# Where the mixer's output product keeps its incoming weights and its reloaded activations

## The chip, the cores and the metric

The kernel runs on one core of a Trainium2 chip. A core has a matrix engine (PE, with its weight loads listed apart as PEld), a vector engine (DVE), a scalar engine (ACT), GpSimd (POOL) and SyncE (SP), which here only issues DMAs. Each engine takes its own instructions in the order in which the program has them; between engines there are semaphores. On-chip memory is SBUF (128 partitions) and PSUM, into which PE writes. The metric is the device time of one execution in microseconds (us).

## The reference

One inference step of a two-layer decoder, on 512 prompt rows and 64 sample rows (576 columns here, in two halves of 288), with the same float32 weights. Layer 0 runs two mixers side by side, an RWKV-7 time mixer (8 heads) and a retention (8 heads), and adds their joint output product to the residual:

```python
y = jnp.concatenate([ya, yb], axis=-1).astype(x.dtype) @ w_out
x = layer_norm(ALPHA * x + y, ln1_g[l], ln1_b[l])
x = layer_norm(ALPHA * x + sqrelu_mlp(x, w_up[l], w_down[l]), ln2_g[l], ln2_b[l])
```

Layer 1 has a gated short convolution as its mixer and the same MLP. Outputs are both sequences and the new states. The product `@ w_out` (1024 x 1024) is what this document is about.

## The kernel before

**Products.** Every float32 operand is split into a high part and a rest (`hi` by a cast on ACT, `lo` by a subtraction on DVE or POOL), and one product is three matmuls, hi x hi, hi x lo and lo x hi (`mm3`, L152 to L154).

**The stage.** The mixers run as twelve generators that `drive` steps in a written order, `SCHEDULE`, with a priority for each step: the projections (0), preparation, staging, inverse, scan and output of four pairs of RWKV heads (1 to 6), their sample rows (7), four pairs of retention heads in a front and a back half (8 to 10), and the output product `wout` (11). A planner at build time then lists each engine's instructions by these priorities and by the times at which its cost model has their inputs ready. So the order on an engine depends on what an instruction has to wait for in the plan.

**The sets.** Two sets of tiles hold what a pair of RWKV heads works on: `ls` (9 x 3 x 64 values per partition, of which `la` and `sv` are views), `lr` (2 x 9 x 2 x 64), `uv` and small ones (`new_set`). Pairs 0 and 2 use the first set, pairs 1 and 3 the second. After pair 2 nothing in the mixers uses the first set any more. The scan's products at L907 are the last that read its `la`.

**The output product** (class `Wout`). The 1024 inputs come as eight tiles y0 to y7 of 128 x 576: y0 to y3 from the RWKV pairs, y4 to y7 from the retention pairs (`ret0` to `ret3`). y0 and y1 are stored in DRAM as Y0 and Y1 and loaded again. `WP` says which inputs go together and what they wait for:

- part 0: y0, y1, y2, after the projections and pair 2 (`ya2`);
- then `means`, which loads the weights of inputs 6 and 7 (eight loads, summed on DVE, L1363), and then those of input 7 again (four loads), takes the mean off and splits them (L1371 to L1373) for the y7 product of the next stage;
- part 1: y3, y4, y5, after `ya3`, `ret0`, `ret1`; then `center`, which takes the mean off the residual tiles x (products L1385, sixteen subtractions on DVE, L1386);
- part 2: y6, after `ret2`.

In a part, each input is cast (L1397, ACT) and its rest taken (L1398, POOL). Then for each of eight blocks m of 128 outputs the weights are loaded by SP (`weights`, L1340 or L1343), cast (L1346, ACT) and subtracted (L1347, POOL), multiplied into two PSUM tiles `wa`, one for each half of the columns, and added to x on DVE (L1413, L1415). Part 2 runs four `weights` for two blocks each.

Where these tiles live: a weight load goes to `wr`, of which pool `wq` has two, its parts to `wh` and `wl` (shown as h and l in the profile), two each. A place is free again when the cast and the subtraction that read it are done. Y0 and Y1 are loaded into `stg` (L1395), one tile, through which all spills of the projections go to DRAM as well (L1061 to L1063). Pool `wq` lies in memory that held the projections' inputs, and is open once these are read for the last time.

**The next stage.** When the mixers' pools close, new ones open on their memory: `raw3` for incoming weights, `wspa` for split ones, `tmp`, and `hp`, which holds constants, the split y7 (`T.hs[7]`, L1599 and L1600) and later activations. In a partition, the sets have bytes 131,264 to 175,808 and `hp` has 91,424 to 156,992. The y7 product and the first layer norm's sums (L283 to L294) follow; the y7 product uses PSUM that `center` leaves.

**Queues.** SP issues, in its order, the weights of the projections and of the output product, spills, reloads, the small copies of the inverse (L811, L814), and the trunk's weights (L59). POOL issues the residual x (L1504, eight loads) when the projections are through.

The functions that the diff touches and their callers, with line numbers of the profile:

Of the kernel before, what the change touches and what calls it, by code (L numbers as in the profile page):

```python
# [10 lines left out]
F32 = mybir.dt.float32  # L11
F32R = mybir.dt.float32r
# [4 lines left out]
P = 128  # L17
NT = 576
# [6 lines left out]
class Trunk:  # L25
    def __init__(self, tc, w_all, wbufs=9, rawbufs=3, ahead=5):
        self.tc, self.nc, self.w_all = tc, tc.nc, w_all
        self.ahead = ahead
        self.nu = w_all.shape[0]
        self.raw, self.split = {}, {}  # L30
        self.loaded = self.done = 0
        self.halves = False
        self.tb, self.wb = 8, 8
        self.cap = 2 * self.nu - 1
        self.pairs = set()
        self.allocs = 0
        self.chunk = 8
        self.spots = {}
        self.gate = []
        self.gated = 0  # L40
        self.direct = False
        self.kfirst = True
        self.half = None
# [1282 lines left out]
class Wout:  # L1326


    def __init__(self, T, w):
        self.T, self.nc, self.w = T, T.nc, w  # L1330
        self.w7, self.less = [], {}
        self.y = [None] * 8

    def weights(self, m, k0, n):

        t = self.wq.tile([P, 2, P], F32, tag='wr', name='wr', bufs=2)
        b = self.less.get(k0)
        if b is None:
            t = t[:, 0:n]
            self.nc.sync.dma_start(t.rearrange('p m c -> p (m c)'), self.w[30 + m, :, P * k0:P * (k0 + n)])  # L1340
        else:
            n = 2
            self.nc.sync.dma_start(t, self.w[30 + m:32 + m, :, P * k0:P * (k0 + 1)].rearrange('m p c -> p m c'))  # L1343
            self.nc.scalar.activation(t, t, AF.Identity, bias=b)
        hi, lo = (self.wq.tile([P, 2, P], F32R, tag=f'w{c}', name=c, bufs=2)[:, 0:n] for c in 'hl')
        self.nc.scalar.copy(hi, t)  # L1346
        self.nc.gpsimd.tensor_tensor(out=lo, in0=t, in1=hi.bitcast(F32), op=ALU.subtract)  # L1347
        return hi, lo

    def means(self):  # L1350


        nc = self.nc

        def load(k, m):
            t = self.wq.tile([P, 2, P], F32, tag='wr', name='wr', bufs=2)
            nc.sync.dma_start(t, self.w[30 + m:32 + m, :, P * k:P * (k + 1)].rearrange('m p c -> p m c'))
            return t
        for k in (6, 7):
            s = self.wq.tile([P, 4], F32, name=f's{k}', bufs=1)  # L1360
            for m in range(0, 8, 2):
                t = load(k, m)
                nc.vector.tensor_reduce(out=s[:, m // 2:m // 2 + 1], in_=t, axis=AX.XY, op=ALU.add)  # L1363
            b = self.wq.tile([P, 1], F32, name=f'b{k}', bufs=1)
            nc.vector.tensor_reduce(out=b, in_=s, axis=AX.X, op=ALU.add)
            nc.vector.tensor_scalar(out=b, in0=b, scalar1=-1.0 / 1024, scalar2=None, op0=ALU.mult)
            self.less[k] = b
        for m in range(0, 8, 2):
            t = load(7, m)
            hi, lo = (self.wq.tile([P, 2, P], F32R, name=f'k{c}{m}', bufs=1) for c in 'hl')  # L1370
            nc.scalar.activation(t, t, AF.Identity, bias=b)  # L1371
            nc.scalar.copy(hi, t)
            nc.gpsimd.tensor_tensor(out=lo, in0=t, in1=hi.bitcast(F32), op=ALU.subtract)  # L1373
            self.w7 += [(hi[:, x], lo[:, x]) for x in range(2)]
# [48 lines left out]
def build(tc, i, o, coff):  # L1423
    nc = tc.nc
    T = Trunk(tc, i['w'], ahead=2)
    with ExitStack() as es:
# [9 lines left out]
        with ExitStack() as s1:  # L1436
            M = Mixers(T, i, o, coff)
# [31 lines left out]
            for k in range(KT):  # L1469
                t = (M, M1)[k // 4].lr.rearrange('p a b c d -> p (a b c d)')[:, NT * (k % 4):NT * (k % 4 + 1)]  # L1470
# [94 lines left out]
                    if n == 1: W.center(mxb)  # L1565
            rt = {}
            W = Wout(T, i['w'])
            W.sp, W.stage = M.sp, lambda: M.e('stg')
            RF = copy.copy(R)
            R.mx = (M.mx, mxb)[RMX]  # L1570
            drive(tc, projs(), pres(), stages(), back(0), back(1), back(2), back(3), samples(), ret_fronts(), ret_backs((0, 2)), ret_backs((1, 3)), wout())
# [219 lines left out]
```

## Time and profile before

| what | before |
|---|---|
| median of 3 timed runs | 1565.62 us (1565.36 to 1569.27) |
| profiled execution | 1561.02 us |
| its span, first to last instruction | 1559.2 us |
| mean granted TensorE clock | 0.970 |
| PE busy | 1471.8 us (94%) |
| DVE, ACT, POOL busy | 1073.9, 644.8, 546.1 us |
| last projection's end, first layer norm's first sums | about 353 and 517 us |

The page gives busy time by engine and in forty slices, the chain of work that ended last, and the costliest groups of instructions; other views list stretches of time, waits, and single instructions with what released them. "A <- B" with three numbers is a wait of A for B: us in total, times, the longest. A timeline row is start, length, engine, line, operation, tiles, count, and in brackets the idle time before it with its releaser. In a row of a stretch the engines come as PE, PEld, DVE, ACT, POOL, each with its busy us and its count.

### The profile page before, as it was taken

To read this page: it belongs to the slowest core of one execution; us is meant where nothing else is said; L and a number is where in the kernel's file an instruction comes from. 1 tells how busy PE (TensorE), PEld (TensorE's weight loads), DVE (VectorE), ACT (ScalarE), POOL (GpSimd) and SP (SyncE) were. 2 spreads that over 40 slices of the span, in tenths; PEclk is the share of its full clock that TensorE was granted. 3 is DMA by queue.
4 is the path that set the end of the run, shared out by engine and by line. 5 is a ranking of instruction groups with operands and counts; after the bars stand their busy time and mean duration, and the time that the engine had idled before them with its cause. 6 is when DMAs were issued, how large, how long until landed. Compare 5 with 4: busy or idle time off the path is not lost.

```text
span 1559.2 us, 29833 instructions
## 1 busy us (share of the span) xinstructions
PE 1471.8 (94%) x11744; PEld 1421.0 (91%) x11744; DVE 1073.9 (69%) x2040; ACT 644.8 (41%) x1355; POOL 546.1 (35%) x619
## 2 busy tenths in 40 slices
PE   6999999998888999999999988999998999999995
PEld 6999898987777889999999988899998999999995
DVE  4656766765756994755747779899799475574755
ACT  4434323332233761432525445444366243251533
POOL 2032213345432350211203466555573030221355
PEclk9999999999979999999999999999999999999998
DMA  5333234435223032241422402222303223132211
GB/s 170 98 97 91 86 96 134 140 92 164 84 73 130 12 104 77 68 131 55 123 68 82 137 14 68 82 78 101 122 1 110 81 72 119 55 122 69 90 60 61
DMA packets 73244, 141.08 MB, mean 90 GB/s; under 512 B 21744, under 2 KB 33248, under 8 KB 73104
## 3 DMA queue, kind: packets, MB, share of 16 engines
q1 hardware_dynamic: 70272, 130.74, 26.8%
q0 software_dynamic: 1536, 5.57, 1.1%
q10 hardware_dynamic: 1296, 2.86, 0.5%
q8 instruction: 92, 1.51, 0.4%
q14 instruction: 48, 0.39, 0.1%
HBM read 125.44 MB, written 13.70 MB: 89 GB/s over the span
## 4 chain that ended last, share of the span: by engine, by line
PE 73%; DVE 11%; DMA 5%; issue 4%; POOL 4%; ACT 2%; SPq 1%; DVEq 0%; ACTq 0%; POOLq 0%
PE acc L152 20%; PE acc L153 20%; PE acc L154 20%; DVE wl L78 3%; PE mx L835 2%; DMA raw<-in_w 2%; DMA wr<-in_w 1%; DVE u L341 1%; PE mx L732 1%; PE wa L152 1%; PE wa L154 1%; DVE hl L78 1%; PE wa L153 1%; PE mx L574 1%; POOL ts L1643 1%
## 5 line engine op out<-in xcount | busy, mean ns | idle before, releaser
L77 ACT CAST wh<-raw 128x512 fp32r<-128x512 f32 x440 | 252.7, 618 | 420.7 <-PE acc L153 267.8
L78 DVE TENSOR_TENSOR wl<-raw,wh 128x512 fp32r<-128x512 f32 x440 | 333.6, 790 | 41.9 <-ACT wh L77 35.1
L153 PE MATMUL acc<-hl,wh 128*128 128x288 f32 x1180 | 348.9, 297 | 0.0
L154 PE MATMUL acc<-hh,wl 128*128 128x288 f32 x1180 | 348.6, 296 | 0.0
L152 PE MATMUL acc<-hh,wh 128*128 128x288 f32 x1180 | 346.3, 297 | 2.0 <-DVE ta L205 1.8
L152 PEld LDWEIGHTS acc<-hh,wh 128*128 128x128 f32 x1180 | 221.2, 188 | 2.9 <-DVE ta L205 2.0
L153 PEld LDWEIGHTS acc<-hl,wh 128*128 128x128 f32 x1180 | 222.2, 188 | 0.5
L154 PEld LDWEIGHTS acc<-hh,wl 128*128 128x128 f32 x1180 | 222.2, 188 | 0.3
L152 PE MATMUL acc<-xh,wh 128*128 128x288 f32 x480 | 147.5, 309 | 14.5 <-ACT xh L1472 12.8
L123 POOL TENSOR_TENSOR s<-raw 128x512 f32<-128x512 f32 x37 | 53.1, 1435 | 268.6 <-DMA raw<-in_w 205.4
L153 PE MATMUL acc<-xl,wh 128*128 128x288 f32 x480 | 145.6, 304 | 0.0
L154 PE MATMUL acc<-xh,wl 128*128 128x288 f32 x480 | 145.5, 303 | 0.0
L153 PE MATMUL acc<-lt,wh 128*128 128x288 f32 x444 | 131.2, 296 | 4.7 <-DVE lt L78 4.7
L154 PE MATMUL acc<-ht,wl 128*128 128x288 f32 x444 | 131.5, 296 | 0.9 <-DVE wl L78 0.9
L152 PE MATMUL acc<-ht,wh 128*128 128x288 f32 x444 | 131.0, 295 | 0.0
L123 POOL TENSOR_TENSOR raw<-raw 128x512 f32<-128x512 f32 x37 | 54.9, 1485 | 160.6 <-DVE raw L123 106.7
L152 PEld LDWEIGHTS acc<-xh,wh 128*128 128x128 f32 x480 | 90.7, 190 | 17.9 <-ACT xh L1472 13.2
L152 PE MATMUL acc<-ho,wh 128*128 128x288 f32 x352 | 104.7, 298 | 0.5 <-DVE tb L205 0.5
L154 PE MATMUL acc<-ho,wl 128*128 128x288 f32 x352 | 105.0, 299 | 0.0
L153 PE MATMUL acc<-lo,wh 128*128 128x288 f32 x352 | 105.0, 298 | 0.0
L153 PEld LDWEIGHTS acc<-xl,wh 128*128 128x128 f32 x480 | 90.9, 189 | 2.5 <-DVE xl L1473 0.7
L154 PEld LDWEIGHTS acc<-xh,wl 128*128 128x128 f32 x480 | 91.0, 190 | 1.5 <-issue 0.2
(485 smaller groups left out, 3478.4 us busy)
## 6 DMA issues: line engine op xcount, KB each, us to landing
raw<-in_w SPq DMA_DIRECT2D x160, 512.0 KB, 3.6
raw<-in_w SPq DMA_DIRECT2D x60, 256.0 KB, 2.9
wr<-in_w SPq DMA_DIRECT2D x32, 128.0 KB, 2.2
A<-stg SPq DMA_DIRECT2D x9, 288.0 KB, 2.4
x<-in_x POOLq DMA_DIRECT2D x8, 288.0 KB, 7.8
out_y<-x SPq DMA_DIRECT2D x16, 144.0 KB, 1.8
kr<-A SPq DMA_DIRECT2D x6, 288.0 KB, 2.7
lr<-in_x ACTq DMA_DIRECT2D x4, 288.0 KB
```

What stands on the lines that cost most here:

```text
L77: a = self.nc.scalar.copy(hi[:, s], src[:, s])
L78: b = self.nc.vector.tensor_tensor(out=lo[:, s], in0=src[:, s], in1=hi[:, s].bitcast(F32), op=ALU.subtract)
L123: tt = lambda e, o, x, y, op: e.tensor_tensor(out=o, in0=x, in1=y, op=op)
L152: nc.tensor.matmul(acc, lhsT=hi, rhs=xh, start=first, stop=False)
L153: nc.tensor.matmul(acc, lhsT=hi, rhs=xl, start=False, stop=False)
L154: nc.tensor.matmul(acc, lhsT=lo, rhs=xh, start=False, stop=last)
L341: nc.vector.tensor_tensor(out=u, in0=r, in1=mn, op=ALU.subtract)
L574: self.nc.tensor.matmul(ps, lhsT=lhsT, rhs=rhs[:, o:o + n], start=True, stop=True)
L732: nc.tensor.matmul(both[h][:, i], lhsT=b3[q, c, h:h + 2].rearrange('p s t -> p (s t)'), rhs=la[q, c], start=True, stop=True)
L835: nc.tensor.matmul(ps[:, i], lhsT=bd(self.mb if n < 3 else self.Y0, j + i), rhs=v[:, j + i], start=True, stop=True)
L1643: (nc.vector if n in SUMV else nc.gpsimd).tensor_tensor(out=t(n), in0=a, in1=b, op=ALU.subtract)
```

## The change

The output product gets places in the first set's tiles. `slot()` cuts the set's `ls` into six pieces of 256 values (pieces of chunks 0 to 7; chunk 8 lies behind them) and hands them out in turn, to `weights` and to the loads of `means` alike: each load takes the next piece, whoever had it. `stage()` cuts the first 1152 values of `lr` into two tiles of 576, one each for Y0 and Y1. The two `wr` tiles go, and the split halves h and l get three tiles each in place of two, so `wq` keeps its size. `stg` is left to the spills. What is computed, and every instruction, stays.

```diff
@@ class Wout
         self.w7, self.less = [], {}
+        self.slots = self.staged = 0
         self.y = [None] * 8
 
+    def slot(self):
+
+        i, self.slots = self.slots % 6, self.slots + 1
+        return self.set.ls.rearrange('p a b c -> p (a b c)')[:, 256 * i:256 * (i + 1)].rearrange('p (m c) -> p m c', c=P)
+
+    def stage(self):
+        i, self.staged = self.staged, self.staged + 1
+        return self.set.lr.rearrange('p a b c d -> p (a b c d)')[:, NT * i:NT * (i + 1)]
+
     def weights(self, m, k0, n):
 
-        t = self.wq.tile([P, 2, P], F32, tag='wr', name='wr', bufs=2)
+        t = self.slot()
...
-        hi, lo = (self.wq.tile([P, 2, P], F32R, tag=f'w{c}', name=c, bufs=2)[:, 0:n] for c in 'hl')
+        hi, lo = (self.wq.tile([P, 2, P], F32R, tag=f'w{c}', name=c, bufs=3)[:, 0:n] for c in 'hl')
...
         def load(k, m):
-            t = self.wq.tile([P, 2, P], F32, tag='wr', name='wr', bufs=2)
+            t = self.slot()
             nc.sync.dma_start(t, self.w[30 + m:32 + m, :, P * k:P * (k + 1)].rearrange('m p c -> p m c'))
@@ build
             W = Wout(T, i['w'])
-            W.sp, W.stage = M.sp, lambda: M.e('stg')
+            W.sp, W.set = M.sp, M
```

## The prediction

> **What bounds the kernel now.** I read the page first, then the busy times by stretch (columns: stretch; length; busy time and count of PE, PEld, DVE, ACT, POOL; granted TensorE clock; DMA share; GB/s), then who waited for whom, the chain of waits, and the timeline of single engines.
>
> ```profile
> span 1559.2 us, 29833 instructions
> PE 73%; DVE 11%; DMA 5%; issue 4%; POOL 4%; ACT 2%; SPq 1%; DVEq 0%; ACTq 0%; POOLq 0%
> 361.00:366.00 5.00, 0.26 (x2) 0.16 (x1) 0.76 (x2) 0.88 (x2) 0.80 (x3) 0.71 0.95 357
> 366.00:376.00 10.00, 10.00 (x92) 9.69 (x92) 4.33 (x7) 2.13 (x8) 3.96 (x4) 0.80 0.27 79
> 416.00:429.00 13.00, 13.00 (x172) 11.44 (x170) 10.64 (x32) 3.10 (x11) 4.74 (x10) 1.00 0.22 69
> 441.00:454.00 13.00, 8.07 (x46) 6.24 (x46) 8.32 (x26) 7.44 (x22) 8.15 (x11) 0.52 0.30 96
> 454.00:463.00 9.00, 9.00 (x41) 8.37 (x41) 2.65 (x9) 0.89 (x3) 1.66 (x4) 0.55 0.11 37
> 463.00:478.00 15.00, 15.00 (x149) 13.48 (x149) 5.95 (x15) 3.51 (x9) 3.87 (x7) 1.00 0.19 61
> 478.00:494.00 16.00, 14.82 (x92) 12.82 (x90) 9.86 (x28) 6.77 (x16) 5.67 (x10) 1.00 0.36 113
> 494.00:501.00 7.00, 2.12 (x9) 1.48 (x9) 7.00 (x19) 5.24 (x12) 1.43 (x2) 0.90 0.61 201
> ```
>
> PE is on 73% of the chain that ends last, and it is full nearly everywhere. The stage that the change touches is an exception: between the last projection (353 us) and the first layer norm (517 us) there are stretches in which PE starves. In 361 to 366 it starts 2 matmuls in 5 us, in 441 to 454 it starts 46 in 13 us, where the 13 us before 429 held 172; in 494 to 501 it starts 9. Behind the second starved stretch the clock is 0.55 for another 9 us, with PE busy throughout. So this stage is bounded by what PE waits for, and by the slow clock that follows such waits. Two chains of waits carry the first two gaps; the third belongs to vector work (below).
>
> ```profile
> PE wa L152 <- ACT hi L1397: 5.6, 2, 4.7
> ACT hi L1397 <- DMA stg<-Y: 9.3, 2, 6.9
> 353.48 3.99 DMA g<-stg
> 357.53 7.56 DMA stg<-Y
> 429.36 2.20 DMA wr<-in_w
> ...
> 450.94 2.29 DMA wr<-in_w
> 453.25 0.41 ACT h L1346
> 453.71 0.61 PE wa L152
> ```
>
> The first gap: the reload of Y0 uses tile `stg`, which must first give up its last spill (g, landed at 357.5). The reload then takes 7.56 us, and the head of PE's queue is a product that waits for its cast. The second gap: the two `wr` buffers take the twelve loads of `means` and then part 1's first weights almost one at a time, from 429.36 to 453.25, and part 1 starts at 453.71.
>
> **The change part by part.** *Activations (two places).* Removed: the wait for `stg`. Moved: two 288 KB loads, earlier on SP. They need Y0 and Y1, stored long before, and the set's `lr`.
>
> ```profile
> 329.86 0.28 PE L907 MATMUL po<-la 64*64 64x64 f32 x4
> 342.06 3.76 SPq L814 DMA_DIRECT2D Y<-d  x8
> 353.04 0.35 SPq L1340 DMA_DIRECT2D wr<-in_w  x1
> 353.31 4.27 POOL L1504 DMA_DIRECT2D x<-in_x  x8 [4.51 <-PE acc L154]
> ```
>
> The row at 329.86 is pair 2's last product over its set; from 330.1 on the six weight places are free too. So both reloads and six weight loads can be issued before 353.04, when the first of them is issued today (the memory of `wr` belongs to the projections' inputs until then). The big x loads (from 353.31), which today run against the Y0 load, come after them. The casts still need `wq`'s memory, so they start at 353. I count all of PE's wait on those casts, 5.6 us (two waits, 4.7 and 0.9): **-5.6**, bounds 0 (another operand is late at the same place) and -5.6. The clock in the 10 us behind is 0.80; at full clock this is 2.0 us less. I take half, **-1.0**, bounds 0 and -2.0, since ret work in it waits for ACT and DMA too.
>
> *Weights (six places, three pairs of split halves).* No instruction is added or taken away. Removed: the wait of a load for the second last user. Each load still has its landing, cast and subtraction; nothing of these gets shorter, they only overlap. Part 1 then starts when its last input is split, not when its weights arrive:
>
> ```profile
> 442.27 0.67 ACT L1397 CAST hi<-tw 128x576 fp32r<-128x576 f32 x1 [0.32 <-DVE tw L1198]
> 443.84 1.40 POOL L1398 TENSOR_TENSOR lo<-tw,hi 128x576 fp32r<-128x576 f32 x1
> ```
>
> That subtraction (y of retention pair 1) ends at 443.84 + 1.40 = 445.24; against 453.71 this is **-8.5**. Bounds: -10.8 (to the end of the last cast, 442.27 + 0.67 = 442.94), and 0, if the retention work of 441 to 454 and not part 1 is what the end waits for. I take -8.5 because from 463 to 494 PE is busy 15.00 of 15 and 14.82 of 16 us: behind the gap the stage is made of PE's own work, and what starts earlier ends earlier.
>
> *Clock.* 9.00 us at 0.55 would be 4.95 at 1.00: -4.05 if the pause before it is filled. Part of it stays (retention operands are late there too), so **-2.0**, bounds 0 and -4.05.
>
> ```profile
> 456.00:459.00 3.00, 3.00 (x16) 3.00 (x16) 0.00 (x0) 0.00 (x0) 0.00 (x0) 0.50 0.08 25
> 459.00:462.00 3.00, 3.00 (x14) 3.00 (x14) 1.12 (x4) 0.41 (x1) 0.18 (x1) 0.50 0.14 46
> ```
>
> [...] The trace has the half clock still in 459 to 462 with PE busy 3.00 of 3 us since 456, so I keep the rows.
>
> *Memory of the set.* Added: the first set is now read until part 2's last weight subtraction, and pool `hp` of the next stage (split y7, constants) lies over part of the sets. A new pool waits for whole old pools, as here, where the first trunk load goes 0.03 us after the last operation on mixer memory (488.12 + 0.76 = 488.88):
>
> ```profile
> 488.12 0.76 DVE L1198 SCALAR_TENSOR_TENSOR y<-y,hd 128x576 f32<-128x576 f32 x1
> 488.91 0.33 SPq L59 DMA_DIRECT2D raw<-in_w  x1
> 488.92 0.67 ACT L1599 CAST hh<-y 128x576 fp32r<-128x576 f32 x1
> 489.68 0.84 DVE L1600 TENSOR_TENSOR hl<-y,hh 128x576 fp32r<-128x576 f32 x1 [0.43 <-ACT hh L1599]
> 494.40 5.91 DVE L1386 TENSOR_TENSOR x<-x,mx 128x288 f32<-128x288 f32 x16
> 500.41 0.58 PE acc L152
> 509.08 0.74 POOL L1347 TENSOR_TENSOR l<-wr,h 128x256 fp32r<-128x256 f32 x1
> 516.59 0.81 DVE L289 TENSOR_TENSOR x<-x,acc 128x288 f32<-128x288 f32 x2
> ```
>
> Today the split of y7 runs at 488.92 to 490.52, and its products start at 500.41, when the 16 centring subtractions leave DVE and PSUM free (494.40 + 5.91 = 500.31). After the change the split waits for the last subtraction of weights. With three pairs of halves only the fourth load must wait, for the products of m = 0 and 1, two adds and 12 products (0.4 and 0.13 us each, rows here and in rival two), some 2.4 us behind 500.31. Cover: DVE has the sixteen adds of part 2 (as the last adds in the fence, 0.81 for two, so 6.5 us) before it misses the y7 products. If the last subtraction stayed at 509.08 + 0.74, the products would begin at 509.82 + 0.67 + 0.84 = 511.33, and 16 adds on DVE of about 0.4 us end at 517.7 or later, 0.3 to 3 us behind today's 517.40. I take **+2.0**, bounds 0 and +3.
>
> *SP and order.* Eight DMAs of 0.35 us move ahead of 353 on SP, past the projections' last weights and spills and the small copies of the inverse: 8 x 0.35 = 2.8 us of SP time. SP is through with those copies at 342.06 + 3.76 = 345.82, and 7.2 us are left to 353.04, so I take 0, bounds 0 and +2.8. On PE, part 0's products become ready earlier and stand among those of pair 3: **+2.0**, bounds 0 and +19 (rival two).
>
> Sum: -5.6 - 1.0 - 8.5 - 2.0 + 2.0 + 0 + 2.0 = **-13.1 us**. The profiled execution took 1561.02 us (span 1559.2 and 1.82 around it), so 1547.9 on its scale. The median of the three timed runs, 1565.62, is 4.6 above it; my prediction goes by the median: 1565.62 - 13.1 = **1552.5 us**.
>
> **Rivals.** *One: only the activations count.* Part 1's early start is swallowed, because its products and the retention pairs share PE, and retention pair 3 (end 488.88) then sets the end. For: the y7 split and the first trunk load both wait for it. Against: the y7 products start 11.5 us after it. Time: -5.6 plus 1.0 of order, 1561.0.
>
> *Two: the products overtake the chain, slower.* Place: PE, 361 to 441. Part 0 is 8 x 3 x 2 x 3 = 144 products; at a step of 0.13 us that is 19 us.
>
> ```profile
> 474.71 0.29 PE L154 MATMUL wa<-hi,l 128*128 128x288 f32 x1
> 474.84 0.29 PE L153 MATMUL wa<-lo,h 128*128 128x288 f32 x1
> ```
>
> Today they trickle in as weights come. If all of them stand ahead of pair 3's inverse and scan and of retention pair 1, they fill the first gap, so that the chain gains nothing there, and the inputs of part 1 come up to 19 us later: 445.24 + 19 = 464.2 against 453.71, +10.5, less the 2.0 of the clock: +8.5, 1574. It decides from 8.5 us of products, some 65, ahead of the chain. For: they were throttled by two buffers only. Against: the written order spreads them between the chain's steps.
>
> *Three: the six places act as one.* If a write to one place waited for readers of the others, every load of part 1 would take its landing (2.20 in the chain above), cast and subtraction one after the other (medians, with 0.390 and 0.724 us, in the rows below): 3.3 us, and 16 of them 53 us against the 40.7 from 453.71 to 494.40 today: +12, 1578. Against: at the start four loads into parts of the same kind of tile (`lr`) are issued in 2.31 us without waiting for each other:
>
> ```profile
> L1346 ACT CAST h<-wr x36: 283/390/407, 355.2 to 509.0; 128x256 fp32r<-128x256 f32 x20, 128x128 fp32r<-128x128 f32 x16
> L1347 POOL TENSOR_TENSOR l<-wr,h x36: 447/724/1203, 360.5 to 510.5; 128x256 fp32r<-128x256 f32 x20, 128x128 fp32r<-128x128 f32 x16
> ...
> 3.52 2.31 POOL L1471 DMA_DIRECT2D lr<-in_x  x4
> ```
>
> **How the numbers follow.** Forecast 0.54, own range 1544 to 1560; better still (all gains at their bounds, -5.6 - 2.0 - 10.8 - 4.05 = -22.45, 1543) 0.04; rival one 0.22; two 0.16; three 0.04. The range leaves out rivals two and three and takes in one with some noise: 1542 to 1568. Under 0.3% (4.7 us) a measurement of this kernel cannot be told from no change. Faster by more: 0.54 + 0.04 and 0.09 of rival one, 0.67. Within: 0.11 of rival one and 0.02 of two, 0.13. Slower: the rest, 0.20.
>
> **What would show it.** Right: reloads of Y0 and Y1 and the first weights issued before 353; no wait of products on their cast at 361 to 366; the twelve loads of `means` in flight several at a time; part 1's first product within 2 us of its last split input; clock 1.0 behind it; the y7 split late, its cost under 3 us. Wrong: part 1's inputs later than 445 (rival two), first products of y7 waiting for their split while DVE idles (memory term), the trunk's start unmoved although part 1 starts earlier (rival one), one load in flight at a time (rival three), or projections that wait for SP before 353.

## The result, and the profile after

| | before | after |
|---|---|---|
| median of the timed runs | 1565.61 us (1565.36 to 1569.27, 4 runs) | 1545.97 us (1545.34 to 1548.84, 4 runs) |
| profiled execution | 1561.02 us | 1545.83 us |
| its span | 1559.2 us | 1544.1 us |
| mean granted TensorE clock | 0.970 | 0.972 |

The ratio is 0.9882, with a 95% interval of 0.9858 to 0.9905: about 18.5 us, or 1.2%, faster. The forecast was 1552.5, so the change gave more than its sum of 13.1 us. The two profiled executions differ by 15.2 us. The rest of the difference of the medians comes from the execution that was profiled before, which lies 4.6 us under its own median; no trace shows those microseconds, so the accounts below are made on the profiles' 15.2. Lines of Wout are ten higher in the kernel after (L1425 is L1415 of before, L1396 is L1386, L1609 is L1599; L1611 where y7 has a memory of its own), and from here on "pair 3" means the last retention pair (`ret3`), which makes y7; its last step is L1198.

The kernel after: the page's span and chain by engine, then the busy times of stretches as before (stretch; length; busy time and count of PE, PEld, DVE, ACT, POOL; granted clock; DMA share; GB/s):

```profile
span 1544.1 us, 29826 instructions
PE 73%; DVE 11%; issue 5%; POOL 4%; DMA 4%; ACT 2%; SPq 1%; DVEq 0%; ACTq 0%; POOLq 0%
```

```profile
361.00:366.00 5.00, 5.00 (x40) 4.71 (x39) 2.77 (x7) 0.77 (x2) 5.00 (x6) 0.83 0.92 331
366.00:376.00 10.00, 10.00 (x110) 9.55 (x109) 6.54 (x12) 3.42 (x12) 5.14 (x8) 1.00 0.49 136
441.00:454.00 13.00, 13.00 (x110) 11.38 (x109) 6.44 (x17) 2.52 (x8) 5.85 (x8) 1.00 0.14 43
454.00:463.00 9.00, 9.00 (x102) 7.87 (x102) 3.37 (x7) 3.63 (x10) 1.22 (x3) 1.00 0.18 52
463.00:478.00 15.00, 9.85 (x78) 8.70 (x73) 11.47 (x27) 3.46 (x10) 5.08 (x7) 0.91 0.08 27
478.00:494.00 16.00, 13.95 (x70) 12.48 (x71) 13.08 (x35) 4.51 (x10) 2.15 (x6) 0.66 0.29 102
```

PE's and DVE's shares of the chain, 73% and 11%, are what they were, so the shares alone tell nothing of this change. The two starved stretches of before are full: 361 to 366 holds 40 matmuls in place of 2, 441 to 454 holds 110 in place of 46, and 454 to 463 runs at a clock of 1.00 in place of 0.55. The clock of 0.83 in 361 to 366 is taken up again below. But a hole has opened further back. From 463 to 478 PE is busy 9.85 of 15 us, where it was full, and from 478 to 494 its clock is 0.66, where it was 1.00.

The kernel after, who waited for whom on PE from 350 to 505 us (total, times, longest), then SP's timeline where the reloads and the first weights are issued, with pair 2's last product over its set on PE:

```profile
PE wa L152 <- DVE x L1425: 6.8, 1, 6.8
```

```profile
316.75 0.38 SPq L1405 DMA_DIRECT2D lr<-Y  x1
317.18 5.30 SPq L1350 DMA_DIRECT2D la<-in_w  x4
322.59 0.51 SPq L1405 DMA_DIRECT2D lr<-Y  x1
332.15 0.28 PE L907 MATMUL po<-la 64*64 64x64 f32 x4
```

The wait on the casts, 5.6 us before, is gone, and the longest wait of PE is a new one: 6.8 us on an add of the output product, which stands behind the centring on DVE. The first reload (L1405, 357.53 us before) and the first weights (L1350, 353.04 before) are issued 41 and 36 us earlier. That is also earlier than the prediction's 330.1: four loads go into their places while pair 2 still reads other parts of the same tile (until 332.15 + 0.28 = 332.43).

The kernel after, timelines. First PE's first product of part 1 and POOL's last split of its inputs; then DVE around the centring, with the last subtraction of weights (POOL), the trunk's first load (SP) and the split of y7 (ACT):

```profile
433.82 0.53 PE L152 MATMUL wa<-hi,h 128*128 128x288 f32 x2
435.42 1.43 POOL L1408 TENSOR_TENSOR lo<-tw,hi 128x576 fp32r<-128x576 f32 x1
```

```profile
472.76 0.64 DVE L585 TENSOR_TENSOR rsa<-rsy 128x10 f32<-128x10 f32 x1
473.32 5.91 DVE L1396 TENSOR_TENSOR x<-x,mx 128x288 f32<-128x288 f32 x16
479.52 0.15 DVE L586 SCALAR_TENSOR_TENSOR rsa<-hv,rsa 128x10 f32<-128x10 f32 x1
...
481.80 0.73 POOL L1357 TENSOR_TENSOR l<-la,h 128x256 fp32r<-128x256 f32 x1 [8.42 <-ACT h L1356]
487.08 0.75 DVE L1198 SCALAR_TENSOR_TENSOR y<-y,hd 128x576 f32<-128x576 f32 x1
487.86 1.29 SPq L59 DMA_DIRECT2D raw<-in_w  x3
487.91 0.67 ACT L1609 CAST hh<-y 128x576 fp32r<-128x576 f32 x1 [2.11 <-issue]
...
503.04 0.81 DVE L289 TENSOR_TENSOR x<-x,acc 128x288 f32<-128x288 f32 x2
507.47 2.64 DVE L311 SCALAR_TENSOR_TENSOR x<-x,par,pq 128x288 f32<-128x288 f32 x6
```

For comparison, the first layer norm's first output in the kernel before:

```profile
522.08 3.49 DVE L311 SCALAR_TENSOR_TENSOR x<-x,par,pq 128x288 f32<-128x288 f32 x8
```

These rows give the account of the whole change:

| us | before | after | difference |
|---|---|---|---|
| last split of part 1's inputs ends | 445.24 | 436.85 | -8.4 |
| part 1's first product | 453.71 | 433.82 | -19.9 |
| centring begins | 494.40 | 473.32 | -21.1 |
| pair 3's last step (L1198) ends | 488.88 | 487.83 | -1.0 |
| last add of the y7 product ends | 517.40 | 503.85 | -13.5 |
| first layer norm's first output | 522.08 | 507.47 | -14.6 |
| span | 1559.2 | 1544.1 | -15.1 |

Behind the first layer norm nothing changes: 1559.2 - 522.08 = 1037.1 us before and 1544.1 - 507.47 = 1036.6 after. So the gain is made ahead of it. It is 21 us at the centring, and 6.5 of these are lost again on the way to the layer norm. The rows of DVE show where a part of it goes: pair 3's inverse root has begun (L585, 472.76), then DVE works through all sixteen centring subtractions (473.32 to 479.23) before it takes the next step of that root (L586, 479.52). Pair 3 ends at 487.83, hardly earlier than before, and the trunk's first load and the split of y7 go 0.03 and 0.08 us behind it. The chain of work that ended last bears this out. In the kernel after it runs from the centring over pair 3's last step to the trunk's first load:

```profile
487.08 0.75 DVE y L1198
487.86 3.70 DMA raw<-in_w
```

In the kernel before it runs over the last adds of the output product, and 0.05 us behind them to the layer norm's first sums (L283, 516.73):

```profile
515.94 0.74 DVE x L1415 x2
```

### The profile page after: what moved, and what is told of

Its sections match the earlier page's. It is cut to its first block, busy times and chain, and to the rows that moved or that the text cites. A ratio compares the mean times of both kernels' runs of the same rounds, so it can differ in the third digit from the quotient of the medians.

```text
span 1544.1 us, 29826 instructions
## 1 busy us (share of the span) xinstructions
PE 1464.9 (95%) x11744; PEld 1414.5 (92%) x11744; DVE 1072.2 (69%) x2040; ACT 643.6 (42%) x1355; POOL 547.9 (35%) x619
## 4 chain that ended last, share of the span: by engine, by line
PE 73%; DVE 11%; issue 5%; POOL 4%; DMA 4%; ACT 2%; SPq 1%; DVEq 0%; ACTq 0%; POOLq 0%
PE acc L152 20%; PE acc L153 20%; PE acc L154 20%; DVE wl L78 3%; PE mx L835 2%; DMA raw<-in_w 1%; POOL x L255 1%; DVE u L341 1%; PE mx L732 1%; POOL ts L1653 1%; PE mx L574 1%; PE wa L152 1%; ACT wh L77 1%; POOL ln L273 1%; PE mx L524 1%
## 5 line engine op out<-in xcount | busy, mean ns | idle before, releaser
L78 DVE TENSOR_TENSOR wl<-raw,wh 128x512 fp32r<-128x512 f32 x440 | 334.0, 791 | 42.0 <-ACT wh L77 35.0
L152 PE MATMUL acc<-hh,wh 128*128 128x288 f32 x1180 | 346.2, 297 | 1.9 <-DVE ta L205 1.8
L152 PEld LDWEIGHTS acc<-hh,wh 128*128 128x128 f32 x1180 | 221.0, 188 | 2.8 <-DVE ta L205 2.0
L152 PE MATMUL acc<-xh,wh 128*128 128x288 f32 x480 | 147.7, 309 | 14.1 <-ACT xh L1482 12.4
L152 PE MATMUL acc<-ht,wh 128*128 128x288 f32 x444 | 131.3, 296 | 0.1
L152 PEld LDWEIGHTS acc<-xh,wh 128*128 128x128 f32 x480 | 90.9, 190 | 17.7 <-ACT xh L1482 12.7
L152 PE MATMUL acc<-ho,wh 128*128 128x288 f32 x352 | 104.6, 297 | 0.1
```

The source lines that it names most:

```text
L78: b = self.nc.vector.tensor_tensor(out=lo[:, s], in0=src[:, s], in1=hi[:, s].bitcast(F32), op=ALU.subtract)
L152: nc.tensor.matmul(acc, lhsT=hi, rhs=xh, start=first, stop=False)
```

## The experiments

Each kernel was timed against the kernel before on the same chip (its medians there: 1565.61 us for the kernel after in the second row, 1564.84 for the four rows behind it, 1563.81 for the next four, 1564.30 for the last four). All compute the whole result; none leaves work out. The last columns are read from the timelines of one execution each, as in the table above: part 1's first product, the end of pair 3's last step, the end of the output product's last add, the first layer norm's first output.

| kernel | median us | ratio, 95% interval | part 1 | pair 3 | last add | norm |
|---|---|---|---|---|---|---|
| before | | 1 | 453.71 | 488.88 | 516.67 | 522.08 |
| after | 1545.97 | 0.9882 (0.9858 to 0.9905) | 433.82 | 487.83 | 499.62 | 507.47 |
| activations alone | 1555.72 | 0.9946 (0.9929 to 0.9964) | 449.12 | 483.92 | 511.56 | 516.97 |
| weights alone | 1553.51 | 0.9923 (0.9904 to 0.9942) | 441.70 | 499.04 | 506.34 | 515.90 |
| two places | 1559.99 | 0.9967 (0.9951 to 0.9982) | 453.55 | 489.38 | 517.55 | 523.00 |
| pair 3 first | 1541.14 | 0.9856 (0.9836 to 0.9875) | 433.24 | 478.92 | 496.82 | 502.29 |
| two pairs of halves | 1554.70 | 0.9936 (0.9911 to 0.9961) | 438.77 | 493.42 | 507.17 | 513.82 |
| pair 3 first, own memory | 1543.32 | 0.9868 (0.9839 to 0.9897) | 434.66 | 481.00 | 501.01 | 506.44 |
| two places, own memory | 1555.93 | 0.9948 (0.9927 to 0.9969) | 451.24 | 487.49 | 514.03 | 519.45 |
| pair 3 first, on before | 1565.21 | 1.0003 (0.9985 to 1.0020) | 456.67 | 486.14 | 520.15 | 525.55 |
| four places | 1555.30 | 0.9942 (0.9923 to 0.9961) | 443.42 | 499.98 | 511.55 | 519.75 |
| three own buffers, on before | 1556.24 | 0.9951 (0.9931 to 0.9970) | 447.36 | 493.74 | 513.17 | 518.58 |
| after, beside | 1545.90 | 0.9883 (0.9865 to 0.9901) | 435.80 | 488.51 | 500.20 | 508.05 |
| pair 3 first, beside | 1541.22 | 0.9855 (0.9834 to 0.9877) | 432.21 | 479.93 | 497.86 | 503.33 |

**One half of the change at a time.** The kernel before with the two activation places only; `wr` and the h and l tiles stay as they were:

```diff
+    def stage(self):
+        i, self.staged = self.staged, self.staged + 1
+        return self.set.lr.rearrange('p a b c d -> p (a b c d)')[:, NT * i:NT * (i + 1)]
...
-            W.sp, W.stage = M.sp, lambda: M.e('stg')
+            W.sp, W.set = M.sp, M
```

> The changed kernel with the weights put back into the two wr tiles and two pairs of split halves; Y0 and Y1 still go to the first set. By the sum of the prediction, the wait on the casts at 361 to 366 goes and the chain of weight loads between part 0 and part 1 stays: 1565.6 - 5.6 - 1.0 + about 1 of order = 1560, part 1's first product about 448. If the activations carry most of the gain: under 1555. If the weights carry all of it: 1565.

The kernel before with the weight places (`slot` in `weights` and `means`) and the third pair of halves only; `stg` serves the reloads as before:

```diff
-            W.sp, W.stage = M.sp, lambda: M.e('stg')
+            W.sp, W.set, W.stage = M.sp, M, lambda: M.e('stg')
...
-            t = self.wq.tile([P, 2, P], F32, tag='wr', name='wr', bufs=2)
+            t = self.slot()
...
-        hi, lo = (self.wq.tile([P, 2, P], F32R, tag=f'w{c}', name=c, bufs=2)[:, 0:n] for c in 'hl')
+        hi, lo = (self.wq.tile([P, 2, P], F32R, tag=f'w{c}', name=c, bufs=3)[:, 0:n] for c in 'hl')
```

> The changed kernel with Y0 and Y1 loaded through stg again; six weight places and three pairs of split halves stay. By the sum, the first gap (about 5 us of PE at 361) stays and the second goes: 1546.0 + 6 = 1552 to 1554. If both halves remove the same wait, so that one alone is enough: 1546 to 1548. If the weights alone do little: above 1560.

Activations alone, POOL's last split of part 1's inputs and PE's first product of part 1; then the same rows of weights alone:

```profile
439.22 1.40 POOL L1408 TENSOR_TENSOR lo<-tw,hi 128x576 fp32r<-128x576 f32 x1
449.12 0.61 PE L152 MATMUL wa<-hi,h 128*128 128x288 f32 x1 [0.61 <-ACT h L1356]
```

```profile
441.70 0.53 PE L152 MATMUL wa<-hi,h 128*128 128x288 f32 x2 [1.10 <-ACT hi L1407]
444.67 1.41 POOL L1408 TENSOR_TENSOR lo<-tw,hi 128x576 fp32r<-128x576 f32 x1 [0.53 <-ACT hi L1407]
```

By the ratios the activations alone give 8.4 us and the weights alone 12.0; together they would be 20.4, and the change gave 18.5, which the intervals cannot tell apart. So the halves work on different waits and nearly add. The weights alone came out as expected (1552 to 1554). The activations alone, expected at 1560, gave more: 1555.72, just above the 1555 that was to mean that they carry most of the gain. With the activations alone the inputs are split at 440.62, 4.6 us earlier, but the first product still comes 8.5 us behind them, on the cast of its weights. With the weights alone the inputs are as late as before (446.08), and part 1 starts ahead of that, at 441.70, with the products of its first input, whose weights lie ready. The first gap is still there: PE's products wait 4.1 us for casts of inputs (L1407).

**How many places.** The kernel after with two places in turn; in the other kernel the 2 is a 4:

```diff
-        i, self.slots = self.slots % 6, self.slots + 1
+        i, self.slots = self.slots % 2, self.slots + 1
```

> The changed kernel with two weight places in the first set in place of six; three pairs of split halves and the places for Y0 and Y1 stay. If the number of places is what counts, the twelve loads of means and the first weights of part 1 go one or two at a time again and part 1 starts some 8 us later: 1546.0 + 8 = 1554 or more. If it is the place (free before the projections end) that counts: 1546 to 1548.

> The kernel after with four places used in turn in place of six; three pairs of split weights. Two places gave 1560.0, six 1546.0, two pairs at six places 1554.7. Theory: the lead comes from weight blocks that lie loaded and split ahead of the products, and a place is given back only when both its copies are made; with three pairs of copies behind them four places are nearly enough: 1546 to 1551, part 1's first product at 434 to 438 us. Rival: the means' twelve loads need all six places (each is taken for a reduction or a split that waits for its turn on its engine), so four give the middle between two and six: 1552 to 1556, part 1's first product at 441 us or later.

Part 1's first product goes with the number: 453.55 with two places, 443.42 with four, 433.82 with six. With two, part 1 stands where it was before; its inputs are split at 444.94, so of the early activations nothing is left there in this profile, and the whole is 0.33% faster. Four places stood nearer to two than the theory had it; the rival's middle (1552 to 1556, 441 us or later) is what was measured. Two places also show the memory term of the prediction, on POOL, ACT and DVE:

```profile
488.62 0.76 DVE L1198 SCALAR_TENSOR_TENSOR y<-y,hd 128x576 f32<-128x576 f32 x1 [2.42 <-ACT hd L1005]
501.03 0.41 ACT L1356 CAST h<-la 128x256 fp32r<-128x256 f32 x1 [3.45 <-PE wa L153]
501.52 0.73 POOL L1357 TENSOR_TENSOR l<-la,h 128x256 fp32r<-128x256 f32 x1 [7.74 <-ACT h L1356]
502.31 0.10 POOL L1599 MEMSET ep<- 128x1 f32 x1
502.95 0.67 ACT L1609 CAST hh<-y 128x576 fp32r<-128x576 f32 x1
```

Pair 3 ends at 489.38, and the split of y7 begins only at 502.95. The last cast of weights waits 3.45 us for the products that hold its copy and comes at 501.03, the last subtraction ends at 502.25, and only then do constants (L1599) and the split (L1609) get memory that lies on the set.

**What that wait costs.** The kernel with two places, the split of y7 in a pool of its own, which does not lie on the sets:

```diff
+            hp0 = pool('hp0', 1, s2)
+            h7 = (hp0.tile([P, NT], F32R, name='hh7'), hp0.tile([P, NT], F32R, name='hl7'))
             T.pools([pool('raw3', RB, s2)], wsp, pool('acc', 6, s2, space=PSUM), pool('misc', 2, s2, space=PSUM), pool('tmp', 1, s2))
...
-            T.hs = [(hp.tile([P, NT], F32R, name=f'hh{k}'), hp.tile([P, NT], F32R, name=f'hl{k}')) for k in range(KT)]
+            T.hs = [(hp.tile([P, NT], F32R, name=f'hh{k}'), hp.tile([P, NT], F32R, name=f'hl{k}')) for k in range(KT - 1)] + [h7]
```

> The kernel with two places, and the same two tiles in a pool of their own. With two places the split began at 502.95 us, 13.6 us behind the last normalisation's end at 489.38. Theory: that wait is the set's release and costs the end something: the split begins at 489.4 to 489.8 and the time falls by 2 to 6 us from 1560.0. Rival: it is hidden behind the output product's own last adds (517.55 us there, 516.67 in the kernel before), so the split moves by 13 us and the time stays at 1559 to 1561.

```profile
486.73 0.76 DVE L1198 SCALAR_TENSOR_TENSOR y<-y,hd 128x576 f32<-128x576 f32 x1 [2.54 <-ACT hd L1005]
489.27 0.66 ACT L1611 CAST hh<-y 128x576 fp32r<-128x576 f32 x1
```

The split now begins at 489.27, 1.8 us behind pair 3, so the wait was the memory's. The median falls by 4.1 us (by the ratios 3.0), inside the theory's 2 to 6, but the two intervals overlap (0.9951 to 0.9982 and 0.9927 to 0.9969), and in both kernels the layer norm stands 5.4 us behind the output product's last add. The planner also ordered other work differently: pair 3 itself ends 1.9 us earlier. That the wait existed is shown; its price, 3 to 4 us, is not settled. This kernel also answers another question. It differs from activations alone by the third pair of halves and by where its two places and the split of y7 lie, and it takes as long: 1555.93 against 1555.72. So early memory for the weights and a third pair give nothing that can be told from noise as long as there are only two places.

**The third pair of halves.** The kernel after with two pairs:

```diff
-        hi, lo = (self.wq.tile([P, 2, P], F32R, tag=f'w{c}', name=c, bufs=3)[:, 0:n] for c in 'hl')
+        hi, lo = (self.wq.tile([P, 2, P], F32R, tag=f'w{c}', name=c, bufs=2)[:, 0:n] for c in 'hl')
```

> The kernel after with two pairs of split weights in place of three; six places as in the kernel after. Theory: the lead of the output product comes from the six places, which let the weights of the first products of part 1 lie ready; with a second pair the split of a third block waits for the first block's products, which follow each other anyway, so the time stays at 1546 to 1549 and part 1's first product stays at 433 to 436 us. Rival: the third pair carries the change, because without it the splitting of part 1's first weights waits for the products of part 0 and runs in step with them as before; then part 1's first product goes back to about 440 to 445 and the time to 1551 to 1556.

The theory fell. The time is 1554.70, 8.7 us above the kernel after, which is the rival's number, although part 1's first product (438.77) went only half the way back to the rival's 440 to 445. Who waited for whom on POOL from 361 to 480 us, with two pairs, then in the kernel after:

```profile
POOL l L1357 <- PE wa L154: 16.9, 7, 4.2
```

```profile
POOL l L1357 <- PE wa L153: 8.5, 3, 5.5
```

With two pairs the subtractions of weights wait 16.9 us for products, with three 9.0 (these 8.5, and 0.5 on L152). A place comes free only when its subtraction is done, so six places behind two pairs would be held up as well. That is argued and not shown: the waits of the same subtractions for their casts go the other way, from 11.9 to 17.5 us, and all their waits together are the same (28.8 and 28.9). The times say less about the buffers than part 1's start does. On top of the early activations (1555.72), six places behind two pairs (1554.70), four behind three pairs (1555.30) and two behind three pairs with a memory of their own (1555.93) give nothing that the intervals can tell from noise; six behind three pairs give 1545.97. In the first two of these part 1 does start earlier than with the activations alone (438.77 and 443.42 against 449.12), but in the new plans pair 3 ends 10 and 16 us later (493.42 and 499.98 against 483.92), and the layer norm comes some 20 us behind it. So how much of the time places and pairs each bring is open.

**More buffers without early memory.** The kernel before with three `wr` buffers, in both places where they are taken:

```diff
-        t = self.wq.tile([P, 2, P], F32, tag='wr', name='wr', bufs=2)
+        t = self.wq.tile([P, 2, P], F32, tag='wr', name='wr', bufs=3)
```

> The kernel before with three buffers of its own for incoming weight blocks in place of two, in the pool that it has (from 353 us on); nothing lies in the set. Theory: the number of blocks under way is what counts, the early memory only for the activations; a third buffer then gives 2 to 4 us: 1561 to 1563. Rival: with two pairs of split weights behind them a third buffer only lets one more block wait, so 1563.5 to 1566, and part 1's first product stays at 452 to 454 us.

One more buffer of 1 KB in a partition gives 8.1 us by the medians (0.9951, 0.9931 to 0.9970) and 5.0 by the spans of the profiled executions (1559.2 and 1554.2), more than either side expected (1561 to 1563, and 1563.5 or more); part 1's first product comes at 447.36 and the layer norm at 518.58. So a good part of what the weights' half gives on its own (12.0) needs no set and no early load, only more blocks under way. Whether it adds to the activations' half was not run.

**Pair 3 first.** The kernel after, with the seven last steps of the generator that runs the back half of pairs 1 and 3 moved ahead in the written order:

```diff
 SCHEDULE
-    (10, 130712), (10, 130980), (10, 131382), (10, 131382), (10, 131650), (10, 132053), (10, 132187)
+    (10, 127010), (10, 127110), (10, 127210), (10, 127310), (10, 127410), (10, 127510), (10, 127610)
```

> The changed kernel with the last seven steps of the second retention generator (the end of pair 3, priorities 130712 to 132187) written ahead of part 1's last five blocks (127010 to 127610); the same instructions. In the changed kernel's profile the last step of pair 3 on DVE ends at 487.8, some 8 us behind the sixteen centring subtractions (479.2), and the trunk's first weight load waits for it. If pair 3's end now sets the stage's end, it comes 5 to 8 us earlier and the time is 1538 to 1541. If part 2's adds or the y7 adds on DVE set it: 1544 to 1546.

DVE, with the split of y7 (ACT) and the last subtraction of weights (POOL):

```profile
470.37 1.68 DVE L997 TENSOR_TENSOR hd<-hd,hv 128x640 f32<-128x640 f32 x1
471.97 5.91 DVE L1396 TENSOR_TENSOR x<-x,mx 128x288 f32<-128x288 f32 x16
478.17 0.75 DVE L1198 SCALAR_TENSOR_TENSOR y<-y,hd 128x576 f32<-128x576 f32 x1
480.75 0.73 POOL L1357 TENSOR_TENSOR l<-la,h 128x256 fp32r<-128x256 f32 x1 [7.43 <-ACT h L1356]
481.52 0.67 ACT L1609 CAST hh<-y 128x576 fp32r<-128x576 f32 x1 [0.84 <-POOL l L1357]
502.29 3.50 DVE L311 SCALAR_TENSOR_TENSOR x<-x,par,pq 128x288 f32<-128x288 f32 x8
```

The root is done and multiplied in (L997) before the centring, pair 3 ends at 478.92, 8.9 us earlier than in the kernel after, and the layer norm comes 5.2 us earlier: 1541.14 us, the fastest version and 0.1 us outside the 1538 to 1541 expected. Not all of the 5.2 us is pair 3's. The layer norm now comes 5.5 us behind the output product's last add in place of 7.8, which is 2.4 us, and the last add itself comes 2.8 us earlier. Half of these 2.8 stand already where the centring begins (471.97 against 473.32). One difference ahead of it is the clock from 361 to 366, 0.83 in the kernel after and 1.00 here, with PE busy 5.00 of 5 us in both. The same seven steps were then moved in the kernel before:

> The kernel before with pair 3's last step moved ahead in the written order in the same way, and nothing else. Theory: pair 3's end became a bound only through the change; before, the output product's last adds at 516.67 us were behind it, so the time stays within 0.3% of 1564.8 (1561 to 1568). Rival: pair 3 was a bound beside the output product already, and moving it ahead gives 4 to 5 us here too, as it does on the kernel after (1546.0 to 1541.1).

There pair 3 also ends earlier, at 486.14 in place of 488.88, and the time does not change (1.0003, 0.9985 to 1.0020), as the theory had it. So pair 3 became a bound only through the change. In pair 3 first, the split of y7 waits 2.6 us behind pair 3, until the last subtraction of weights (480.75 + 0.73 = 481.48). The memory of its own was tried there too (same edit as above):

> The kernel with pair 3 first, and the two tiles of the seventh input's split for the stage behind in a pool of their own that does not lie on the mixer's sets. In the kernel with pair 3 first the split began at 481.52 us, 2.6 us behind the last normalisation's end at 478.92. Theory (the memory term of the prediction): these 2.6 us are the wait for the last reading of a place in the set; the split then begins within 0.3 us of the last normalisation's end, and the time is 1538.5 to 1541, 0 to 2.6 us below 1541.1. Rival: the products of the last part and the adds behind them set the end there, so the split moves and nothing behind it does: 1541 within 1.

The split follows pair 3 by 0.04 us, as the theory had it, but pair 3 itself ended 2.1 us later in the new plan (481.00), and the time, 1543.32, lies outside both ranges and cannot be told from 1541.14. What 2.6 us of this wait cost is open.

**After and pair 3 first, side by side.** Both unchanged:

> The kernel after, unchanged, beside the next run on the same chip, so that both stand against the same runs of the kernel before: 1545 to 1547.

> The kernel after with pair 3's last step moved ahead, the same as the run with pair 3 first, beside the kernel after. Theory: pair 3's end was the bound of the stage's end, and 4 to 5 us come back: 1540.5 to 1542.5, with an interval that lies below that of the kernel after. Rival: the gain of the first comparison was within its scatter (1543.3 with the own memory): 1543 to 1546, intervals that overlap.

They give 1545.90 and 1541.22, 4.7 us apart, as in the first comparison (1545.97 and 1541.14). The intervals of the two ratios still overlap a little (0.9865 to 0.9901, 0.9834 to 0.9877), so the theory's condition that they lie apart is not met. For the gain speak that it came out the same twice, and that the layer norm moved by 4.7 us (508.05 to 503.33) in the profiles of this pair. Here too 2.4 us of it is the shorter way from the last add to the layer norm (7.9 and 5.5). The other 2.3 is the last add, and these 2.3 are there in full where the centring begins (475.30 and 472.99). The mean granted clock of the two profiled executions differs too, 0.974 and 0.978 (0.972 and 0.976 in the first comparison). By this account pair 3's end is worth 2.4 us both times. What the rest of the gain comes from is open: the other order of work in the new plan, or the clock.

**What the columns say together.** In eight of the kernels (before among them: 516.67 and 522.08) the layer norm's first output comes 5.4 to 5.5 us behind the output product's last add: before, activations alone, two places with and without own memory, pair 3 first (both times) and with own memory, pair 3 first on before, three own buffers. In the kernel after, with two pairs, and with four places, that distance is 7.8, 6.7 and 8.2 us, and the norm comes 19.6, 20.4 and 19.8 us behind pair 3 (7.9 and 19.5 where the kernel after ran beside the other). In weights alone (9.6 and 16.9) pair 3 is late too, and the 16.9 shows that the way behind it has no fixed length. So there are two ends to this stage, and whichever is later sets the start of everything behind it. In the kernel after it is pair 3, by 7.8 - 5.4 = 2.4 us. Behind pair 3 DVE has no pause there from 490.75 to 503.85 us: it does the adds of the y7 product (L289), the subtractions of the trunk's first weights (L78), whose loads waited for pair 3, and among them the last adds of part 2.

## Why the prediction was right, and which terms were wrong

**The sign and the mechanism held.** The two starved stretches were the place of the gain, and the waits named for them were its cause. Against the profiles the sum was 13.1 and the result 15.2. That the sum came so near is in part luck. Its terms ahead of the centring add up to -5.6 - 1.0 - 8.5 - 2.0 + 2.0 = -15.1, and the centring moved by -21.1. Behind it the sum has +2.0, and 6.5 us were lost. So an error of 6.0 and one of 4.5 stand on opposite sides. The prediction's reason to count on no such loss, that behind the gap "the stage is made of PE's own work, and what starts earlier ends earlier", failed: from 463 to 478 PE is busy 9.85 of 15 us in the kernel after.

**Activations: -5.6 right, -1.0 not borne out as a whole.** Part 1's inputs are split 8.4 us earlier with the whole change, 4.6 with the activations alone; 6.6 lies between. No product waits on a cast from 361 to 366 any more. The clock in 366 to 376 is 1.00 in place of 0.80. But a slow stretch stands ahead of it now, from 359 to 363 in the kernel after:

```profile
359.00:363.00 4.00, 4.00 (x24) 3.71 (x23) 1.31 (x5) 0.12 (x1) 3.94 (x5) 0.57 1.01 377
```

At full clock these 4 us of work would be 0.43 x 4 = 1.7 us shorter, an estimate from this row, so of the 2.0 us some 0.3 are left over the two stretches. The clock falls here without a pause of PE: it is busy 28.00 of 28 us from 350 to 378. With the activations alone and in pair 3 first the clock from 361 to 366 is 1.00 (0.83 in the kernel after), with PE busy 5.00 of 5 us in all three, and no run here shows why.

**Part 1's start: -8.5, too small, and its reason too narrow.** The prediction let part 1 begin when its last input is split. With the weights ready it begins with its first input: at 433.82, 3.0 us ahead of the end of the last split at 436.85, and with the weights alone 4.4 us ahead. The bound of -10.8 was wrong for the same reason: the weights alone moved the start by 12.0. With the activations' -6.6 the forecast for the start was -15.1; it moved by 19.9. The row of "within 2 us of its last split input" is thus met on the other side. Nor are the twelve loads of `means` issued any closer together: from first to last they take 19.6 us on SP (403.72 to 423.36) and took 17.7 (429.36 to 447.01). What changed is that they begin 25.6 us earlier, since the last weights of part 0 are issued by 403.37 in place of 425.04, and that part 1's first three weight loads go among them (412.87, 415.88 and 420.75; the first of them went at 450.94 before).

**The third pair was given no price of its own.** The prediction spoke of it only where it delays the reading of the set. Without it 8.5 of the 18.5 us are gone, by the ratios.

**Clock: -2.0.** In 454 to 463 the whole 4.05 came back (1.00). But the clock falls at another pause, that of PE during the centring. Stretches of 3 us behind the centring, before and then after:

```profile
500.00:503.00 3.00, 2.59 (x11) 2.62 (x12) 3.00 (x6) 1.04 (x3) 0.00 (x0) 0.50 0.06 10
503.00:506.00 3.00, 3.00 (x14) 3.00 (x14) 2.19 (x6) 0.44 (x1) 0.00 (x0) 0.50 0.79 294
506.00:509.00 3.00, 3.00 (x23) 3.00 (x22) 2.73 (x8) 1.23 (x4) 1.17 (x1) 0.92 0.60 227
```

```profile
477.00:480.00 3.00, 0.35 (x1) 0.35 (x2) 3.00 (x11) 0.00 (x0) 0.00 (x0) 0.50 0.00 0
480.00:483.00 3.00, 3.00 (x12) 2.57 (x11) 2.78 (x11) 0.41 (x1) 0.91 (x2) 0.50 0.00 0
483.00:486.00 3.00, 2.60 (x11) 2.03 (x11) 1.14 (x4) 1.07 (x2) 0.39 (x1) 0.50 0.07 22
486.00:489.00 3.00, 3.00 (x12) 2.53 (x12) 2.52 (x6) 0.67 (x1) 0.38 (x3) 0.50 0.09 14
489.00:492.00 3.00, 3.00 (x24) 3.00 (x23) 2.63 (x7) 0.36 (x1) 0.00 (x0) 1.00 0.91 321
```

Before, it was half from 500 to 506. After, it stays half from 477 to 489, though PE works again from 479.65: 9.4 us. So the pause moved forward with the centring, and its slow stretch grew from 6 to 9.4 us, which gives back 0.5 x 3.4 = 1.7 us, an estimate from these rows, of the clock's gain. In 454 to 463 of the kernel before the clock was 0.55 with PE busy 9.00 of 9 us, which is about 8 us at the half clock, an estimate from that row. So the stretches here are 6, 8 and 9.4 us long, and no run shows what sets their length.

**Memory: +2.0, nothing in this kernel, real beside it.** The last subtraction of weights ends at 481.80 + 0.73 = 482.53, 5.3 us before pair 3. So the split had nothing to wait for. The cover named in the prediction (the adds of part 2) was not the one; pair 3's late end was. Where pair 3 is early (2.6 us) or the places are few (13.6 us) the wait appears as described.

**Order: +2.0.** The cost is there, but on DVE instead of PE. Part 1's inputs came earlier, not up to 19 us later, so rival two is out. The sixteen subtractions that came between the steps of pair 3 held up the end, and cost 2.4 us by the columns above. The change of order gave 4.7, but of these, too, only 2.4 can be put down to the end of pair 3.

**Rival one** had half of the truth: pair 3 does set the end of the stage, at 487.83 against 488.88, and the trunk's first load goes 1.05 us earlier only, which the prediction had named as a sign for this rival. Its time (1561.0) was wrong, because the path from pair 3 to the layer norm was not as long as before: 522.08 - 488.88 = 33.2 us then, 19.6 now. In the kernel before most of that path was the output product's own work. **Rival three** is out: the first weights are issued as four loads in one row of 5.30 us (317.18), up to 15 us ahead of pair 2's last product over the same tile (332.15), so a load does not wait for the readers of the other places. And each two places more gave part 1 a lead of 10 us.

## What to carry to other kernels

A stage that starves can be fed from tiles that an earlier stage has left; count the places by the whole row from load to last reader, since with the activations early only six places and three pairs together gave time (10 us), and try first what one more plain buffer gives (here 8 us of 18.5). When a long chain is shortened, look for the next end of the stage in the same trace: here it stood a few microseconds behind, and the steps that a batch of sixteen subtractions had held up were cheap to move. Where the next stage opens on memory that is still in use, it waits for the last reader; here that showed only with two places (13.6 us) and with pair 3 early (2.6 us).

## What was not expected of the hardware

The time that TensorE works at the half clock after a pause differs from case to case. After the centring it was 9.4 us in the kernel after (479.65 to 489), behind a pause of 6.8 us. In the kernel before the pause was 4.2 us and the slow stretch some 6 us (500.41 to between 506 and 507), with no gap in PE's work. With pair 3 first the pause was 4.5 us, and the clock was back at about 483, 4.7 us after PE's return at 478.30. The last kernel's longest wait on PE and its stretches of 3 us:

```profile
PE wa L152 <- DVE x L1425: 5.1, 3, 4.5
```

```profile
478.00:481.00 3.00, 2.70 (x10) 2.23 (x10) 2.19 (x5) 0.40 (x1) 0.25 (x1) 0.50 0.30 68
481.00:484.00 3.00, 3.00 (x17) 3.00 (x17) 2.36 (x5) 2.02 (x4) 1.38 (x5) 0.66 1.01 410
484.00:487.00 3.00, 3.00 (x25) 3.00 (x24) 3.00 (x7) 2.88 (x6) 0.00 (x0) 1.00 0.53 179
```

In the longest stretch PE had short gaps (2.60 of 3 us in 483 to 486). Whether these or the longer pause kept the clock down, no run here tells apart. The other two, 6 and 4.7 us behind almost equal pauses and without gaps, show that the pause alone does not set the length. And from 359 to 363 in the kernel after the clock was 0.57 with no pause at all: PE was busy 28.00 of 28 us from 350 to 378.
